# A planner's port waits between VectorE and GpSimd, its model of the DMA wires, and its due times

## The chip, the cores and the metric

One core of one Trainium2 chip. The metric is the device time of one execution in microseconds, the median of several runs. The engines are named as in the profile: PE is TensorE, PEld its weight loads, DVE is VectorE, ACT is ScalarE, POOL is GpSimd, SP is SyncE, which here only issues DMAs.

## What is computed

One layer of a hybrid encoder block on 512 tokens of width 1024, all in float32: three groups of attention heads behind one input projection, one output projection, a gated MLP with a causal convolution of width 3, and a gated per-layer embedding. Cut to what matters:

```python
def reference(x, p, ...):                       # x: (1, 512, 1024)
    h = x
    hn = rms_norm(h, ln_mix[0])
    z = hn @ w_in[0]                            # 1024 x 3590
    (q1, q2, k1, k2, va, qf, kf, vf, fg, qc, kc, vc) = split(z)
    # QK RMS norm of all heads, then
    o_a = diff_attention(q1, q2, k1, k2, va, lam, ...)   # 4 heads, two softmaxes each, ALiBi
    o_b = forgetting_attention(qf, kf, vf, log_f)        # 6 heads, cumulative log forget gate
    o_c = chunk_attention(qc, kc, vc, rel_bias)          # 6 heads, relative position bias
    h = h + concat([o_a, o_b, o_c]) @ w_out[0]
    h = h + conv_gated_mlp(rms_norm(h, ln_ffn[0]), w_up, conv_w, conv_b, w_down)   # d_ff 2816
    gate = sigmoid(rms_norm(h, ln_ple[0]) @ w_ple_gate[0])
    return h + (p[0] @ w_ple_proj[0]) * gate
```

## The kernel before

**Arithmetic.** Every float32 product is made of three fast ones: an operand is split into a rounded part (`whi`, `Th`, made by ScalarE with a cast) and the rest (`wlo`, `Tl`, made by DVE or POOL with a subtraction), and `mm3` issues hi*hi, hi*lo and lo*hi into one PSUM bank. So each weight tile of 128 x 768 takes a load by SP, a cast of ScalarE and a subtraction over two SBUF operands before PE can use it. The tiles stand in rings: 4 to 6 raw ones (`wraw`), 7 or 8 of `whi` and of `wlo`; a load waits until the subtraction has let go of the raw tile. Some sums of weights are made beforehand, on POOL by `tensor_tensor` (`sum_of`, line 1383) or by a POOL DMA that accumulates (`add_of`, line 1376).

**First part** (to line 1132, about the first 280 us): the input projection in ten parts of 4 token tiles, between them the attention of the pairs of heads. POOL has short steps in these chains: the power for the RMS norm (`rs`, in `qk_sums`, line 689), the moves of halves of `q` and `k` that scores wait for (`move`, line 712, called by `split_q` and `split_k`), the scaling of probabilities (`e`). DVE makes the splits, the masked scores with their minimum (`e` with its accumulator `st`, in `softmax_map`, line 852), reciprocals and evacuations. **Second part** (from line 1140): output projection's end, the MLP, with a saving of products for two blocks at a time that needs sums of weights and of activations (`up_seven`, line 1571; `down_weights`, line 1428), and the gate with the output.

**The planner.** Nothing is issued where it is written. While a plan is open (`PLAN`), every call on an engine becomes an `Op` of `Plan` (line 124) with the tiles that it reads and writes. `price` (line 184) gives it a duration; `op.port` (line 216) marks what uses the SBUF port that DVE and POOL share: every POOL operation but a DMA, and a DVE `tensor_scalar`, `tensor_tensor` or `scalar_tensor_tensor` with no operand in PSUM. `due` (line 225) gives PE operations due times by their place plus a shift of their group out of the table `SHIFT`, and from these, backwards, all others. `solve` (line 236) then plays the engines in time: at each step the engine that can start first takes the ready operation that is due first. `emit` (line 305) issues the operations in the order found; each engine runs its own in that order, and data dependencies become semaphores. All instructions therefore carry one line, L357, in the profile.

What the change touches in it:

- A port operation is planned only after the other engine's last one (`when`, line 247, over `held`). In the second plan POOL is planned 0.1 us later still (`late`, the fifth argument at line 1140), and in `emit` (line 313) a POOL operation over 0.6 us that follows a DVE port operation in the order gets a real semaphore wait on it (`behind`). The first plan (line 595) has `late` 0 and no such waits. DVE never waits for POOL on account of the port.
- DMAs share one wire in the plan, at 0.37 MB/us for those of SP, 0.105 for those of POOL, one after the other.
- `SURE` is 0.1: PE takes first what has been ready that long. `STICK` and `turns` keep transposes in bunches, and a lone transpose is charged 0.08 us.

Of the kernel before, what the change touches and what calls it, by code (L numbers as in the profile page):

```python
# [41 lines left out]
for _i in range(3):  # L42
# [5 lines left out]
AHEAD = 2  # L48
# [75 lines left out]
class Plan:  # L124
# [5 lines left out]
    def __init__(self, clock, there=(), mem=None, fresh=0.0, late=0.0):  # L130
        self.group, self.loaded, self.fresh, self.late = "first", set(), fresh, late
        self.clock, self.there, self.ops, self.mem = clock, [(v.tensor.name, self.region(v), t) for v, t in there], [], mem or {}

    @staticmethod
    def region(v):
        size = 2 if v.dtype == BF16 else 4
        (row, pn), *rest = [tuple(x) for x in v.ap]
        if v.tensor.space == bass.MemoryType.DRAM and v.tensor.name not in STAND_INS:
            return 0, 1, v.offset * size, (v.offset + (pn - 1) * row + sum((n - 1) * st for st, n in rest) + 1) * size
        p0, c0 = divmod(v.offset, row)  # L140
        return p0, p0 + pn, c0 * size, (c0 + sum((n - 1) * st for st, n in rest) + 1) * size
# [42 lines left out]
    def price(self, op):  # L184
# [4 lines left out]
        op.move, op.turns = 0, op.name == "transpose"  # L189
# [29 lines left out]
    LONG, STICK = 0.6, 2.0  # L219
    HW, SW, AT_ONCE = 0.37e6, 0.105e6, 8  # L220
    SURE, AHEAD, MUCH, WAIT = 0.1, 1.0, 2.0, 0.6
# [3 lines left out]
    def due(self, shift):  # L225
# [5 lines left out]
        for op in reversed(self.ops):  # L231
            if op.eng.name != "pe":
                spent = op.busy + op.lag + 0.05 + (op.move / self.HW + 2.0 if op.move else 0.0)
                op.dl = min([q.dl for q in op.next], default=t) - spent

    def solve(self):
# [6 lines left out]
        wire, out, order = 0.0, {"sp": [], "pool": []}, []  # L243
        turns, alone = False, False
        held = {"dve": 0.0, "pool": 0.0}
        other = {"dve": "pool", "pool": "dve"}
        when = lambda q: max(q.at, held[other[q.eng.name]] + (self.late if q.eng.name == "pool" else 0.0)) if q.port else q.at
        rank = lambda q: (q.dl, q.pos)
        while True:
            best = None  # L250
            for e in self.ENGINES:
                if free[e]:
                    t = max(clock[e], min(when(q) for q in free[e]))
                    if best is None or t < best[0]:
                        best = t, e
            if best is None:
# [3 lines left out]
            if e == "pe":  # L260
                can = [q for q in can if q.at + self.SURE <= t] or can
            op = min(can, key=rank)
            if e == "pe" and op.turns != turns:
                same = [q for q in can if q.turns == turns and q.dl < op.dl + self.STICK]
                if same and (turns or sum(q.turns and q.dl < op.dl + self.STICK for q in can) < 2 or min(q.dl for q in same) < op.dl + self.STICK / 2):
                    op = min(same, key=rank)
# [12 lines left out]
            if e == "pe":  # L279
                busy += 0.08 * (alone and not op.turns)  # L280
                turns, alone = op.turns, op.turns and not turns
            if op.move:
                done = out[e]
                if len(done) >= self.AT_ONCE:
                    t0 = max(t0, done[-self.AT_ONCE])
                wire = max(t0 + 2.0, wire) + op.move / (self.HW if e == "sp" else self.SW)
                op.end = wire + 0.6
                done.append(op.end)
# [7 lines left out]
            for q in op.next:  # L296
                q.left -= 1
                q.at = max(q.at, op.start if e == "pe" and q.eng is op.eng else op.end + self.LEAD[q.eng.name])
                if not q.left:
                    free[q.eng.name].append(q)  # L300
# [4 lines left out]
    def emit(self):  # L305
# [3 lines left out]
        before = None  # L309
        for op in self.choose():  # L310
            op.ins = op.eng.now(op.name, [real(v) for v in op.a], {q: real(v) for q, v in op.k.items()})
            if op.port:
                if before and op.eng.name == "pool" and before.eng.name == "dve" and op.busy > self.LONG and self.late:
# [1744 lines left out]
```

## Time and profile before

| | us |
|---|---|
| median of 3 runs | 708.28 |
| lowest and highest run | 708.25, 709.49 |
| the profiled execution | 707.89 |
| its span, first to last instruction | 706.0 |
| mean granted TensorE clock, share | 0.998 |

The span is shorter than the execution by what lies around the program. In the profile's views each row of a chain or timeline has its start and its length in us; x2 after a name merges two neighbours. A group's row has the busy time, the mean ns of one instruction, the idle time of its engine just before and what ended that. In a row of waits stand the total us, how many times, and the longest. A row by tile gives the shortest, median and longest instruction in ns.

### The profile page before, as it was taken

To read this page: it belongs to the slowest core of one execution; us is meant where nothing else is said; L and a number is where in the kernel's file an instruction comes from. 1 tells how busy PE (TensorE), PEld (TensorE's weight loads), DVE (VectorE), ACT (ScalarE), POOL (GpSimd) and SP (SyncE) were. 2 spreads that over 40 slices of the span, in tenths; PEclk is the share of its full clock that TensorE was granted. 3 is DMA by queue.
4 is the path that set the end of the run, shared out by engine and by line. 5 is a ranking of instruction groups with operands and counts; after the bars stand their busy time and mean duration, and the time that the engine had idled before them with its cause. 6 is when DMAs were issued, how large, how long until landed. Compare 5 with 4: busy or idle time off the path is not lost.

```text
span 706.0 us, 12402 instructions
## 1 busy us (share of the span) xinstructions
PE 690.3 (98%) x4420; PEld 636.4 (90%) x4420; DVE 552.5 (78%) x1126; ACT 408.7 (58%) x781; POOL 300.6 (43%) x403
## 2 busy tenths in 40 slices
PE   7999999999999999999999999999999999999997
PEld 7999999898999888899998999889988888999886
DVE  7679878879788666789888887997877998878722
ACT  6657676565766575666666435665345674536711
POOL 3788677766665452223223334304432203245200
PEclk9999999999999999999999999999999999999999
DMA  9523444423112252584763278651488552204521
GB/s 321 201 83 111 125 117 128 118 60 109 45 61 76 75 124 83 200 244 105 214 159 113 68 186 207 163 162 33 139 211 209 183 168 82 91 32 155 163 85 46
DMA packets 41275, 92.72 MB, mean 131 GB/s; under 512 B 4694, under 2 KB 7510, under 8 KB 41212
## 3 DMA queue, kind: packets, MB, share of 16 engines
q1 hardware_dynamic: 34572, 78.24, 33.1%
q0 software_dynamic: 6352, 13.38, 10.8%
q8 instruction: 35, 0.57, 0.3%
q10 hardware_dynamic: 288, 0.30, 0.1%
q14 instruction: 28, 0.23, 0.1%
HBM read 83.63 MB, written 4.21 MB: 124 GB/s over the span
## 4 chain that ended last, share of the span: by engine, by line
PE 91%; DVE 3%; DMA 2%; ACT 2%; POOL 1%; issue 1%; ACTq 0%; POOLq 0%
PE z L357 46%; PE s L357 22%; PE t L357 16%; PE o L357 7%; DMA wraw<-in_w_up_dram 1%; DVE wlo L357 1%; POOL k L357 1%; POOL q L357 1%; ACT whi L357 1%; DMA zn<-in_w_in_dram 0%; DVE e L357 0%; DVE conv L357 0%; POOL rs L357 0%; ACT e L357 0%; DVE kl L357 0%
## 5 line engine op out<-in xcount | busy, mean ns | idle before, releaser
L357 ACT CAST whi<-wraw 128x768 fp32r<-128x768 f32 (+2 forms) x140 | 106.1, 768 | 59.9 <-POOL wraw L357 11.4
L357 PE MATMUL z<-whi,Th 128*128 128x384 f32 (+2 forms) x356 | 123.4, 351 | 4.5 <-ACT whi L357 4.5
L357 DVE TENSOR_TENSOR wlo<-wraw,whi 128x768 fp32r<-128x768 f32 (+2 forms) x122 | 111.5, 930 | 15.4 <-ACT whi L357 13.6
L357 PE MATMUL z<-wlo,Th 128*128 128x384 f32 (+2 forms) x356 | 123.0, 350 | 0.0
L357 PE MATMUL z<-whi,Tl 128*128 128x384 f32 (+2 forms) x356 | 121.8, 347 | 0.0
L357 PEld LDWEIGHTS z<-whi,Th 128*128 128x128 f32 x356 | 66.9, 189 | 8.0 <-ACT whi L357 4.5
L357 POOL TENSOR_TENSOR wraw<-wraw,wraw 128x256 f32<-128x256 f32 (+1 forms) x22 | 28.3, 1285 | 101.3 <-DVE wlo L357 53.6
L357 PEld LDWEIGHTS z<-wlo,Th 128*128 128x128 f32 x356 | 67.2, 189 | 4.0 <-DVE wlo L357 0.4
L357 PEld LDWEIGHTS z<-whi,Tl 128*128 128x128 f32 x356 | 67.0, 189 | 3.8
L357 ACT ACTIVATE e<-e,st 128x128 f32<-128x128 f32 (+3 forms) x80 | 44.7, 560 | 29.8 <-DVE st L357 29.4
L357 PE MATMUL z<-Th,whi 128*128 128x512 f32 (+1 forms) x156 | 53.2, 346 | 1.4 <-ACT whi L357 1.3
L357 PE MATMUL s<-Th,whi 128*128 128x512 f32 (+1 forms) x156 | 53.3, 345 | 0.6 <-ACT whi L357 0.6
L357 PE MATMUL s<-Th,wlo 128*128 128x512 f32 (+1 forms) x156 | 53.7, 345 | 0.0
L357 PE MATMUL s<-Tl,whi 128*128 128x512 f32 (+1 forms) x156 | 53.6, 345 | 0.0
L357 PE MATMUL z<-Tl,whi 128*128 128x512 f32 (+1 forms) x156 | 53.5, 344 | 0.0
L357 PE MATMUL z<-Th,wlo 128*128 128x512 f32 (+1 forms) x156 | 53.4, 344 | 0.0
L357 POOL TENSOR_TENSOR rs<-rs,nhalf 128x4 f32<-128x4 f32 x40 | 43.5, 1091 | 4.8 <-DVE rs L357 2.3
L357 DVE CUSTOM_DVE_ANT_0 e<-s,bias 128x128 f32<-128x128 f32 (+3 forms) x74 | 33.7, 469 | 12.4 <-PE s L357 7.2
L357 DVE TENSOR_TENSOR conv<-conv,conv 128x512 f32<-128x512 f32 (+1 forms) x31 | 21.0, 691 | 24.0 <-ACT conv L357 23.8
L357 POOL TENSOR_SCALAR e<-e,st 128x512 f32<-128x512 f32 (+3 forms) x48 | 27.2, 576 | 18.1 <-DVE st L357 16.8
L357 PEld LDWEIGHTS z<-Th,whi 128*128 128x128 f32 x156 | 29.1, 188 | 4.8 <-ACT whi L357 1.8
L357 PEld LDWEIGHTS s<-Th,whi 128*128 128x128 f32 x156 | 29.2, 188 | 3.8 <-ACT whi L357 0.8
(352 smaller groups left out, 2152.4 us busy)
## 6 DMA issues: line engine op xcount, KB each, us to landing
wraw<-in_w_up_dram SPq DMA_DIRECT2D x41, 384.0 KB, 4.3
wraw<-in_w_in_dram SPq DMA_DIRECT2D x28, 384.0 KB, 3.7
wraw<-in_w_down_dram SPq DMA_DIRECT2D x16, 384.0 KB, 3.6
whi_again<-in_w_up_dram SPq DMA_DIRECT2D x11, 384.0 KB, 4.5
wraw<-in_w_out_dram SPq DMA_DIRECT2D x16, 256.0 KB, 2.7
wlo_again<-in_w_up_dram SPq DMA_DIRECT2D x10, 384.0 KB, 4.3
wraw<-in_w_up_dram SPq DMA_DIRECT2D x15, 256.0 KB, 4.1
wlo<-wraw POOLq DMA_DIRECT2D x7, 384.0 KB, 4.2
```

Source lines behind the costliest of these rows:

```text
L357: ins = getattr(self.eng, op)(*a, **k)
```

## The change

Both plans get semaphore waits in both directions. In `emit`, a port operation of either engine that lasts over 0.25 us waits for the last port operation that the builder has issued on the other engine before it, unless one of its engine already waited for that same one, and only if the plan starts it before that one's end plus `NEAR` (1.0 us for POOL, 0.6 for DVE). In `solve` a port operation is planned 0.2 us (POOL) or 0.1 us (DVE) after the other engine's end. The fifth argument of `Plan` is now `sure`, PE's margin of readiness: 0.15 in the first plan, still 0.1 in the second, whose call is unchanged. DMAs are played as two queues whose transfers are served in order, alone at 0.334 (SP) or 0.164 MB/us (POOL), at 0.143 and 0.078 when both are at work; at most 8 are on the way in a queue. The bunching of transposes and the charge for a lone one go. All values of `SHIFT` are new.

```diff
 SHIFT = {
-    "first": -11.4, "in1_0": -0.3, "in1_1": -25, "in1_2": -2.7, "A0a": -6.5, ...
+    "first": -23.2, "in1_0": -20, "in1_1": -10.4, "A0a": -14.9, ...
...
-    def __init__(self, clock, there=(), mem=None, fresh=0.0, late=0.0):
+    def __init__(self, clock, there=(), mem=None, fresh=0.0, sure=0.15):
...
-    LONG, STICK = 0.6, 2.0
-    HW, SW, AT_ONCE = 0.37e6, 0.105e6, 8
-    SURE, AHEAD, MUCH, WAIT = 0.1, 1.0, 2.0, 0.6
+    SHORT, HANDED, NEAR = 0.25, {"pool": 0.2, "dve": 0.1}, {"pool": 1.0, "dve": 0.6}
+    RATE = {("sp",): {"sp": 0.334e6}, ("pool",): {"pool": 0.164e6}, ("sp", "pool"): {"sp": 0.143e6, "pool": 0.078e6}}
+    SENT, ARRIVED, AT_ONCE = {"sp": 1.46, "pool": 1.49}, 0.58, 8
+    AHEAD, MUCH, WAIT = 1.0, 2.0, 0.6
...
-        when = lambda q: max(q.at, held[other[q.eng.name]] + (self.late if q.eng.name == "pool" else 0.0)) if q.port else q.at
+        def when(q):
+            if q.port:
+                return max(q.at, held[other[q.eng.name]] + self.HANDED[q.eng.name])
+            if q.move:
+                return max(q.at, gate[q.eng.name]) if len(wire[q.eng.name]) < self.AT_ONCE else never
+            return q.at
...
+        def landed(until):
+            nonlocal now
+            while now < until:
+                busy = tuple(e for e in wire if wire[e] and wire[e][0][1] <= now)
+                rate = self.RATE.get(busy, {})
...
-                can = [q for q in can if q.at + self.SURE <= t] or can
+                can = [q for q in can if q.at + self.sure <= t] or can
             op = min(can, key=rank)
-            if e == "pe" and op.turns != turns:
-                same = [q for q in can if q.turns == turns and q.dl < op.dl + self.STICK]
...
-            if e == "pe":
-                busy += 0.08 * (alone and not op.turns)
-                turns, alone = op.turns, op.turns and not turns
...
-                if before and op.eng.name == "pool" and before.eng.name == "dve" and op.busy > self.LONG and self.late:
-                    op.eng.behind(op.ins, before.ins)
-                before = op
+                e = op.eng.name
+                d = last["pool" if e == "dve" else "dve"]
+                if d and d is not known[e] and op.busy > self.SHORT and op.start < d.start + d.busy + self.NEAR[e]:
+                    op.eng.behind(op.ins, d.ins)
+                    known[e] = d
+                last[e] = op
```

More of the change, by code (lines that the diff above doesn't have):

```diff
@@ L128 @@
     LEAD = {"act": 0.035, "dve": 0.035, "pool": 0.095, "pe": 0.055, "sp": 0.1}
-    def __init__(self, clock, there=(), mem=None, fresh=0.0, late=0.0):
-        self.group, self.loaded, self.fresh, self.late = "first", set(), fresh, late
+    def __init__(self, clock, there=(), mem=None, fresh=0.0, sure=0.15):
+        self.sure = sure
+        self.group, self.loaded, self.fresh = "first", set(), fresh
         self.clock, self.there, self.ops, self.mem = clock, [(v.tensor.name, self.region(v), t) for v, t in there], [], mem or {}
@@ L137, in region @@
         (row, pn), *rest = [tuple(x) for x in v.ap]
-        if v.tensor.space == bass.MemoryType.DRAM and v.tensor.name not in STAND_INS:
+        if v.tensor.space == bass.MemoryType.DRAM and v.tensor.name not in STAND_INS and v.tensor.name != "out_dram":
             return 0, 1, v.offset * size, (v.offset + (pn - 1) * row + sum((n - 1) * st for st, n in rest) + 1) * size
@@ L188, in price @@
         acc = "accum_out" in k
-        op.move, op.turns = 0, op.name == "transpose"
+        op.move = 0
         if e == "pe":
@@ L232, in due @@
             if op.eng.name != "pe":
-                spent = op.busy + op.lag + 0.05 + (op.move / self.HW + 2.0 if op.move else 0.0)
+                spent = op.busy + op.lag + 0.05 + (op.move / 0.37e6 + 2.0 if op.move else 0.0)
                 op.dl = min([q.dl for q in op.next], default=t) - spent
@@ L242, in solve, with release @@
                 free[op.eng.name].append(op)
-        wire, out, order = 0.0, {"sp": [], "pool": []}, []
-        turns, alone = False, False
+        wire, now, gate, order = {"sp": [], "pool": []}, 0.0, {"sp": 0.0, "pool": 0.0}, []
         held = {"dve": 0.0, "pool": 0.0}
         other = {"dve": "pool", "pool": "dve"}
-        when = lambda q: max(q.at, held[other[q.eng.name]] + (self.late if q.eng.name == "pool" else 0.0)) if q.port else q.at
+        never = 1e18
+        def when(q):
[4 more added lines that the diff above has]
+            return q.at
+        def release(op, e):
+            for q in op.next:
+                q.left -= 1
+                q.at = max(q.at, op.start if e == "pe" and q.eng is op.eng else op.end + self.LEAD[q.eng.name])
+                if not q.left:
+                    free[q.eng.name].append(q)
+        def landed(until):
[3 more added lines that the diff above has]
+                rate = self.RATE.get(busy, {})
+                step, who = until - now, None
+                for e in wire:
+                    if e in rate and wire[e][0][2] / rate[e] <= step:
+                        step, who = wire[e][0][2] / rate[e], e
+                    if wire[e] and e not in rate and wire[e][0][1] - now < step:
+                        step, who = wire[e][0][1] - now, None
+                now = until if step == until - now else now + step
+                for e in rate:
+                    wire[e][0][2] -= rate[e] * step
+                if who:
+                    op = wire[who].pop(0)[0]
+                    op.end = now + self.ARRIVED
+                    if len(wire[who]) + 1 >= self.AT_ONCE:
+                        gate[who] = op.end
+                    return op, who
+            return None
         rank = lambda q: (q.dl, q.pos)
@@ L255, in solve @@
                         best = t, e
+            there = landed(best[0] if best else never) if wire["sp"] or wire["pool"] else None
+            if there:
+                release(*there)
+                continue
             if best is None:
@@ L260, in solve @@
             if e == "pe":
-                can = [q for q in can if q.at + self.SURE <= t] or can
+                can = [q for q in can if q.at + self.sure <= t] or can
             op = min(can, key=rank)
-            if e == "pe" and op.turns != turns:
-                same = [q for q in can if q.turns == turns and q.dl < op.dl + self.STICK]
-                if same and (turns or sum(q.turns and q.dl < op.dl + self.STICK for q in can) < 2 or min(q.dl for q in same) < op.dl + self.STICK / 2):
-                    op = min(same, key=rank)
             if e not in ("pe", "sp"):
@@ L278, in solve @@
             busy = op.busy * (1.85 if e == "pe" and t0 < 8.6 else 1.0)
-            if e == "pe":
-                busy += 0.08 * (alone and not op.turns)
-                turns, alone = op.turns, op.turns and not turns
             if op.move:
[L283 to L288, printed above, removed]
+                wire[e].append([op, t0 + self.SENT[e], op.move])
             else:
@@ L295, in solve @@
             order.append(op)
[L296 to L300, printed above, removed]
+            if not op.move:
+                release(op, e)
         assert len(order) == len(self.ops)
@@ L308, in emit @@
                 d.next.append(op)
-        before = None
+        last, known = {"dve": None, "pool": None}, {"dve": None, "pool": None}
         for op in self.choose():
```

75 rows, old and new, of the table SHIFT are left out of this document.

## The prediction

> **What bounds the kernel now.** I read the page first, then the chain that ended last, then the waits of TensorE (PE) alone, then two halves of the span.
>
> ```profile
> span 706.0 us, 12402 instructions
> PE 690.3 (98%) x4420; PEld 636.4 (90%) x4420; DVE 552.5 (78%) x1126; ACT 408.7 (58%) x781; POOL 300.6 (43%) x403
> ```
> ```profile
> PE 91%; DVE 3%; DMA 2%; ACT 2%; POOL 1%; issue 1%; ACTq 0%; POOLq 0%
> ```
>
> PE is busy for 690.3 of 706.0 us and carries 91% of the chain. So no edit on another engine is worth more than the 15.7 us in which PE is idle, and most of that is out of reach, as the next view shows.
>
> ```profile
> PE z L357 <- ACT whi L357: 5.8, 2, 4.5
> PE s L357 <- POOL k L357: 2.1, 3, 1.3
> PE s L357 <- DVE st L357: 1.3, 2, 1.1
> PE s L357 <- ACT whi L357: 0.6, 1, 0.6
> PE t L357 <- DVE kl L357: 0.2, 1, 0.2
> PE t L357 <- DVE ptl L357: 0.2, 1, 0.2
> PE t L357 <- issue: 0.2, 1, 0.2
> ```
>
> Columns: total us, times, longest. The 4.5 is the start, before the first weights are there; no edit touches it. What lies behind PE's last matmul isn't in this list either. The change can win only the rest: 1.3 + 2.1 + 1.3 + 0.6 + 0.6 = 5.9 us. That is the ceiling, 0.8% of the span.
>
> Two of these waits are collisions of VectorE (DVE) and GpSimd (POOL). First the chain of work around the longest wait for POOL k, the DVE's timeline beside it, and the same POOL operation over the whole run:
>
> ```profile
> 121.78 1.99 POOL q L357
> 123.78 0.59 POOL k L357
> 124.37 0.04 issue
> 124.41 0.74 PE s L357 x4
> ```
> ```profile
> 122.36 0.94 DVE L357 TENSOR_TENSOR wlo<-wraw,whi 128x768 fp32r<-128x768 f32 x1
> ```
> ```profile
> L357 POOL TENSOR_SCALAR q<-ql x20: 611/616/1994, 36.6 to 256.4; 64x512 fp32r<-64x512 f32 x20
> ```
>
> A move of the median 616 ns took 1.99 us, and it ended 0.47 us after DVE's weight split (122.36 + 0.94 = 123.30), though it had begun 0.58 us ahead of it. The scores waited for the next move behind it. The second case is the longest wait for DVE st:
>
> ```profile
> 155.13 3.83 DVE wlo L357 x2
> 158.96 0.26 DVE e L357
> ...
> 159.28 0.73 PE s L357 x2
> ```
> ```profile
> 155.98 2.15 POOL L357 TENSOR_TENSOR wlo<-wraw,whi 128x768 fp32r<-128x768 f32 x1
> ```
> ```profile
> L357 DVE TENSOR_TENSOR wlo<-whi_again,whi 128x768 fp32r<-128x768 f32 x18 | 17.2, 954 | 3.1 <-ACT whi L357 3.0
> ```
>
> The last row is from the groups by shape; its 954 is the mean ns of one split. Two of them should take 1.9 us; beside a POOL subtraction of 2.15 us they took 3.83. So each engine holds the other, in both directions. A third place shows that POOL can lose several times in a row:
>
> ```profile
> 32.27 3.45 POOL L357 TENSOR_TENSOR rs<-rs,nhalf 128x4 f32<-128x4 f32 x1 [0.97 <-DVE rs L357]
> ```
> ```profile
> 32.16 2.69 DVE L357 TENSOR_TENSOR wlo<-wraw,whi 128x768 fp32r<-128x768 f32 x3
> ```
> ```profile
> L357 POOL TENSOR_TENSOR rs<-rs,nhalf x40: 1002/1018/3447, 26.9 to 232.3; 128x4 f32<-128x4 f32 x40
> ```
>
> A power of 1018 ns took 3447, until all three back-to-back splits were through.
>
> **The change, part by part.** *Waits between the two engines.* Until now only a POOL operation over 0.6 us waits, only in the second part, only right behind a DVE port operation. Now each engine's port operation over 0.25 us waits for the other's last one in the builder's order, in both parts, if the plan has it start soon after. It removes no work and adds no pass over data. It decides who goes first: the DVE split at 122.36, if planned behind the moves, no longer overtakes them, and the scores at 124.41 lose their 1.3; the split at 155 either runs first or leaves its place to `e`, and the 1.1 goes. The rest of the POOL k group is 0.8; I take half of it, 0.4, since nothing in the list says which of the two shorter waits come from a held move. Together 1.3 + 1.1 + 0.4 = 2.8. Bounds: 0 (the order stays as it is) and 3.4 (all of both groups).
>
> What a wait costs by itself comes from handoffs that are there already:
>
> ```profile
> 154.59 0.16 DVE L357 RECIPROCAL st<-st 128x1 f32<-128x1 f32 x1 [1.14 <-ACT e L357]
> 154.85 0.37 POOL L357 TENSOR_SCALAR e<-e,st 128x128 f32<-128x128 f32 x1 [0.32 <-DVE st L357]
> ```
> ```profile
> 286.16 0.58 POOL L357 TENSOR_TENSOR rstd<-rstd,nhalf 128x1 f32<-128x1 f32 x1
> 286.77 0.75 DVE L357 SCALAR_TENSOR_TENSOR conv<-h,rstd,pin 128x512 f32<-128x512 f32 x1 [0.35 <-POOL rstd L357]
> ```
>
> From DVE to POOL 154.85 - 154.75 = 0.10 us, from POOL to DVE 286.77 - 286.74 = 0.03. The rule waits at most once for any one operation, so with 403 POOL instructions DVE gets at most 403 new waits, 12 us, against 706.0 - 552.5 = 153.5 us idle; POOL's at most 403 come to 40 us against 405 idle. As sums they are hidden. Uncovered, on a chain such as POOL q, k, PE s, one costs its 0.1.
>
> The dear part is what stands behind a waiting DVE instruction. The DVE runs in order; behind a split that waits for POOL stand the `e` and `st` of the next scores, for which ScalarE and PE wait, and the next split, for which SP's loads wait (SP's waits, then the first 280 us; columns of the latter: PE, weight loads, DVE, ScalarE, POOL, clock, DMA share, GB/s):
>
> ```profile
> SPq L357 <- DVE wlo L357: 304.0, 122, 14.7
> ```
> ```profile
> 0.00:280.00 280.00, 271.56 (x1648) 254.40 (x1649) 219.19 (x629) 180.37 (x427) 177.05 (x275) 1.00 0.37 113
> ```
>
> In the first 280 us DVE has 61 us idle and POOL is busy 177 of 280, so a wait there has cover only if the plan is right about POOL. I charge three new small waits of PE of 0.3 each, +0.9: the handoff's 0.1 and the 0.2 that the shorter wait for DVE st lasts (1.3 - 1.1). Bounds: nothing, and the 1.1 of a real hold at each of some places, which is the rival below.
>
> *Wire rates.* The planner now lets a hardware and a GpSimd queue share the wire and slow each other. The place where this matters is the 0.6 us wait for whi, behind a weight load that the chain shows:
>
> ```profile
> 538.98 5.21 DMA wraw<-in_w_up_dram
> ```
> ```profile
> wraw<-in_w_up_dram SPq DMA_DIRECT2D x41, 384.0 KB, 4.3
> ```
>
> It landed 0.9 us later than the median. Knowing this, the planner can only issue earlier or take PE work in another order, and SP's 304 us of waiting for splits says that a load goes out when a buffer comes free, no sooner. So I count half of the two later whi waits, (1.3 + 0.6) / 2 = 0.9 as a gain; bounds 0 and 1.9, and a loss of one more such wait, 1.3.
>
> *Transposes no longer bunched, and no charge for a lone one.* The rows around a lone transpose, and a bunch of three:
>
> ```profile
> 43.20 0.28 PE L357 MATMUL s<-kl,q 128*128 128x256 f32 x1
> 43.31 0.27 PE L357 MATMUL t<-ident,zn 128*128 128x128 f32 x1
> 43.34 0.42 PE L357 MATMUL z<-whi,Th 128*128 128x384 f32 x1
> 43.60 0.34 PE L357 MATMUL z<-wlo,Th 128*128 128x384 f32 x1
> 43.78 0.34 PE L357 MATMUL z<-whi,Tl 128*128 128x384 f32 x1
> ```
> ```profile
> 122.44 0.49 PE L357 MATMUL t<-ident,e 128*128 128x128 f32 x3
> ```
>
> From 43.20 to 43.60 are 0.40 us. A 384-wide step takes 43.78 - 43.60 = 0.18, the 256-wide one 43.31 - 43.20 = 0.11, which leaves 0.11 for the transpose. In the bunch, with the lone one's 0.27 for the last, one takes (0.49 - 0.27) / 2 = 0.11 as well. So splitting bunches costs nothing that I can see; I take 0. *The readiness margin of 0.15 instead of 0.1 in the first part and the new due times* only reorder; their cost is in the three waits above.
>
> Sum: 707.89 (the profiled execution, 706.0 of it span) - 2.8 - 0.9 + 0.9 = 705.1. The median of the three runs, 708.28, lies 0.39 above the profiled execution, so the forecast is **705.5 us**.
>
> **Rivals.** *The waits only rename the blocking.* Both engines already exclude each other; if the builder's order is the order that happens anyway, or the thresholds catch few of the held pairs, a held instruction becomes a waiting one and PE's list stays: 708.3, at most 0.4 less or more for handoffs. Against it speaks that the move begun at 121.78 was overtaken. [...]
>
> *DVE is held behind a late POOL operation (slower).* A fixed order can't use it when POOL comes late: DVE stands with ready work behind it. Its price is the row at 155: 1.9 us of hold made 1.1 us of PE wait. POOL has 275 instructions in the first 280 us; if six of the waits for them (one in 46) end like this, the time is 708.3 - 2.8 + 6.6 = 712.1; with seven, 713.2. It decides from three on, whose 3.3 eats the 2.8. For it speaks DVE's 78% there (219.19 of 280); against it that nearly all moves and powers keep to their medians (616, 1018), so that the plan can know when POOL is done.
>
> *More than I count goes.* If the new plan clears the whole list, 708.3 - 5.9 = 702.4.
>
> **How the numbers follow.** This kernel's runs can tell about 0.2%, 1.4 us: faster is under 706.9, slower over 709.7. Forecast 0.42; the list cleared 0.10 (0.04 of it under 702.4); renaming 0.12; DVE held 0.36, of which 0.08 over 713.2. So faster 0.52, same 0.12, slower 0.36, and the range 702.4 to 713.2 leaves out 0.12. The forecast's own range is 703.9 to 706.9.
>
> **What would show it.** Right: stretched POOL moves and powers fall to their medians (616, 1018 ns) and DVE's splits to 954; PE's waits for POOL k and DVE st fall from 3.4 to about 1; lone transposes still cost 0.11. Wrong: new lines in which DVE waits for POOL, followed by PE waiting for DVE st, zn or wlo; SP's wait for splits above 304 us; a wait of PE for whi over 1.3. If the list shrinks and the time doesn't, the tail or PE's order took it back.

## The result, and the profile after

| | before | after |
|---|---|---|
| median, us | 708.26 (6 runs, 707.39 to 709.49) | 715.95 (6 runs, 711.46 to 717.21) |
| profiled execution, us | 707.89 | 715.94 |
| its span, us | 706.0 | 714.2 |

The kernel got slower: ratio 1.0098, interval 1.0082 to 1.0114. It is the side of the second rival, above its 712.1.

First the page's head of the changed kernel (all its instructions carry line L386):

```profile
span 714.2 us, 12433 instructions
PE 696.9 (98%) x4420; PEld 639.2 (90%) x4420; DVE 543.6 (76%) x1126; ACT 409.7 (57%) x781; POOL 277.9 (39%) x403
```

DVE is busy 8.9 us less and POOL 22.7 us less than before, for the same instructions: the two no longer hold each other. PE does the same 4420 matmuls and is busy 6.6 us *more*; its idle time rose only from 15.7 to 17.3. So the loss must be looked for inside PE's busy time too. The waits of PE, without the start and four rows of 0.2 or 0.3 (columns: total us, times, longest):

```profile
PE s L386 <- ACT conv L386: 2.9, 1, 2.9
PE t L386 <- DVE wlo L386: 1.3, 1, 1.3
PE z L386 <- ACT Th L386: 0.8, 2, 0.7
PE t L386 <- DVE ptl L386: 0.8, 1, 0.8
PE z L386 <- DVE Tl L386: 0.6, 1, 0.6
PE s L386 <- DVE st L386: 0.5, 2, 0.3
```

The wait for POOL k (2.1) is gone, that for DVE st fell from 1.3 to 0.5, and the later waits for whi (1.3 and 0.6) are gone. In their place stand waits that the kernel before did not have. Now by place. For each matmul I took the time from its start to the start of the next one, less what it takes in an unbroken row (0.117 us for 256 columns, 0.175 for 384, other widths in proportion, 0.109 for a transpose), and summed this by stretch. It is worked out from all of PE's rows in the timeline, so it also holds pauses that are too short for the list of waits:

| stretch, us | before | after |
|---|---|---|
| 0 to 120 | 4.3 | 7.1 |
| 120 to 160 | 4.4 | 1.5 |
| 160 to 280 | 0.6 | 1.7 |
| 280 to 360 | -0.1 | 2.3 |
| 360 to 440 | 0.8 | 0.5 |
| 440 to 480 | 0.0 | 5.1 |
| 480 to 560 | 3.0 | 2.6 |
| 560 to the end | 0.5 | 1.9 |
| all | 13.7 | 22.7 |

The whole difference is 9.0 us; the span grew by only 8.2, because what lies behind PE's last matmul got shorter, from 5.3 to 4.4 us. (The change also has the planner track the output in DRAM by region, in a line that the diff above doesn't show; what shortened the end was not tried.) The stretch with the two collisions that the prediction named gained 2.9. Five of the other seven lose, 360 to 440 and 480 to 560 gain a little; the dearest is 440 to 480. There the timeline shows, POOL first, then DVE, ScalarE and PE (start, length, engine and operation, in brackets the idle time before and what ended it):

```profile
449.71 0.87 POOL L386 DMA_DIRECT2D wraw<-in_w_up_dram  x1 [0.37 <-issue]
454.35 0.73 POOL L386 TENSOR_TENSOR wraw<-wraw 128x256 f32<-128x256 f32 x1 [3.77 <-DMA wraw<-in_w_up_dram]
...
455.11 1.53 DVE L386 SCALAR_TENSOR_TENSOR conv<-conv,cols,conv 128x511 f32<-128x511 f32 x2 [4.75 <-POOL wraw L386]
...
457.28 1.01 ACT L386 CAST ah<-conv 128x512 fp32r<-128x512 f32 x2 [3.22 <-DVE conv L386]
458.62 0.39 PE L386 MATMUL s<-Th,whi 128*128 128x256 f32 x1 [2.85 <-ACT conv L386]
```

Read from the top: a POOL DMA that adds a weight tile to another goes out at 449.71. POOL's next sum needs it and stands 3.77 us. DVE's convolution needs none of these weights, only the turn that the new wait gives it; it stands 4.75 us until POOL's 0.73 us sum is done. ScalarE stands behind the convolution, and PE waits 2.9 us for ScalarE's rounded part. And then the bill goes on. The same execution in short windows (window, its length, PE, weight loads, DVE, ScalarE, POOL busy with counts, granted clock, DMA share, GB/s):

```profile
454.00:458.00 4.00, 1.76 (x13) 1.33 (x12) 2.85 (x5) 0.78 (x3) 0.73 (x1) 1.00 0.50 99
460.00:461.00 1.00, 1.00 (x7) 1.00 (x7) 0.77 (x1) 0.00 (x0) 1.00 (x2) 0.65 0.87 335
461.00:462.00 1.00, 1.00 (x7) 1.00 (x6) 1.00 (x4) 0.00 (x0) 0.02 (x1) 0.50 0.32 30
462.00:463.00 1.00, 1.00 (x7) 1.00 (x7) 0.20 (x1) 0.82 (x1) 0.00 (x0) 0.50 0.89 119
463.00:464.00 1.00, 1.00 (x5) 0.86 (x5) 0.96 (x1) 0.76 (x3) 0.00 (x0) 0.64 1.10 289
464.00:466.00 2.00, 2.00 (x16) 1.83 (x15) 1.30 (x3) 1.51 (x4) 0.84 (x2) 1.00 0.71 213
```

About 1.7 us after PE went on, TensorE's granted clock fell to a half, and from 460.4 on a 256-column step took 0.21 us instead of 0.117. PE counts as wholly busy there and does less: (1 - 0.65) + 0.50 + 0.50 + (1 - 0.64) = 1.7 us lost, so an estimated 1.7 / 0.5 = 3.4 us at half the clock, with no row in the list of waits. The hold cost 2.9 + 1.7, near the 5.1 of this stretch. In e7 below, where DVE doesn't stand behind this sum, the same count gives 0.5 for the stretch.

How often the new waits keep DVE standing behind POOL shows in DVE's list:

```profile
DVE wlo L386 <- POOL wlo_again L386: 7.3, 5, 2.8
DVE wlo L386 <- POOL wraw L386: 5.7, 4, 3.6
DVE conv L386 <- POOL wraw L386: 4.8, 1, 4.8
DVE pin L386 <- POOL wraw L386: 2.6, 2, 1.4
```

These 20.4 us have no counterpart before. All four lines are waits for sums of weights in the second part. Besides the one above, those that seem to reach PE lie at 314, 320 and 543 us: the waits for Tl (0.6), Th (0.7) and wlo (1.3) follow soon after them. No wait in PE's list stands behind the 3.6 at 491 us.

### The profile page after: what moved, and what is told of

The parts are those of the page before. It is cut to its first block, busy times and chain, and to the rows that moved or that the text cites. A ratio compares the mean times of both kernels' runs of the same rounds, so it can differ in the third digit from the quotient of the medians.

```text
span 714.2 us, 12433 instructions
## 1 busy us (share of the span) xinstructions
PE 696.9 (98%) x4420; PEld 639.2 (90%) x4420; DVE 543.6 (76%) x1126; ACT 409.7 (57%) x781; POOL 277.9 (39%) x403
## 5 line engine op out<-in xcount | busy, mean ns | idle before, releaser
L386 ACT CAST whi<-wraw 128x768 fp32r<-128x768 f32 (+2 forms) x140 | 105.8, 769 | 47.5 <-PE s L386 13.3
L386 PE MATMUL z<-whi,Th 128*128 128x384 f32 (+2 forms) x356 | 124.0, 357 | 5.0 <-ACT whi L386 4.5
L386 PE MATMUL z<-wlo,Th 128*128 128x384 f32 (+2 forms) x356 | 122.3, 352 | 0.4 <-DVE V L386 0.3
L386 PE MATMUL z<-whi,Tl 128*128 128x384 f32 (+2 forms) x356 | 122.1, 351 | 0.0
L386 DVE TENSOR_TENSOR wlo<-wraw,whi 128x768 fp32r<-128x768 f32 (+2 forms) x122 | 104.6, 879 | 19.6 <-ACT whi L386 9.6
L386 PEld LDWEIGHTS z<-whi,Th 128*128 128x128 f32 x356 | 67.0, 190 | 9.9 <-ACT whi L386 4.5
L386 PEld LDWEIGHTS z<-wlo,Th 128*128 128x128 f32 x356 | 66.8, 189 | 4.9 <-DVE wlo L386 0.5
L386 PEld LDWEIGHTS z<-whi,Tl 128*128 128x128 f32 x356 | 66.9, 189 | 3.6
L386 PE MATMUL s<-Th,whi 128*128 128x512 f32 (+1 forms) x156 | 54.0, 347 | 2.9 <-ACT conv L386 2.9
L386 PE MATMUL z<-Tl,whi 128*128 128x512 f32 (+1 forms) x156 | 53.6, 346 | 0.6 <-DVE Tl L386 0.6
L386 PE MATMUL z<-Th,whi 128*128 128x512 f32 (+1 forms) x156 | 53.4, 345 | 0.7 <-ACT Th L386 0.7
L386 PE MATMUL s<-Tl,whi 128*128 128x512 f32 (+1 forms) x156 | 53.8, 346 | 0.0
L386 PE MATMUL s<-Th,wlo 128*128 128x512 f32 (+1 forms) x156 | 53.7, 348 | 0.0
L386 PE MATMUL z<-Th,wlo 128*128 128x512 f32 (+1 forms) x156 | 53.6, 345 | 0.0
L386 ACT ACTIVATE e<-e,st 128x256 f32<-128x256 f32 (+3 forms) x80 | 44.7, 561 | 14.7 <-DVE st L386 14.1
L386 POOL TENSOR_TENSOR wraw<-wraw,wraw 128x256 f32<-128x256 f32 (+1 forms) x22 | 27.1, 1241 | 65.5 <-DVE wlo L386 39.7
L386 POOL TENSOR_TENSOR rs<-rs,nhalf 128x4 f32<-128x4 f32 x40 | 40.7, 1019 | 19.9 <-DVE wlo L386 10.1
L386 DVE CUSTOM_DVE_ANT_0 e<-s,bias 128x384 f32<-128x384 f32 (+3 forms) x74 | 33.7, 470 | 8.9 <-PE s L386 7.8
L386 PEld LDWEIGHTS s<-Th,whi 128*128 128x128 f32 x156 | 29.6, 190 | 6.9 <-ACT conv L386 3.7
L386 DVE TENSOR_TENSOR conv<-conv,conv 128x512 f32<-128x512 f32 (+1 forms) x31 | 20.4, 670 | 19.1 <-ACT conv L386 18.8
L386 PEld LDWEIGHTS z<-Th,whi 128*128 128x128 f32 x156 | 29.2, 188 | 4.3 <-ACT Th L386 0.9
L386 PEld LDWEIGHTS z<-Tl,whi 128*128 128x128 f32 x156 | 29.2, 188 | 4.0 <-DVE Tl L386 0.8
```

What stands on the lines that cost most here:

```text
L386: ins = getattr(self.eng, op)(*a, **k)
```

## The experiments

Two theories stood at the start: the new waits cost, because they hold DVE behind POOL sums that come late (in the expectations W); and the new order costs, while the waits only rename a blocking that is there anyway (O). The first runs refuted a half of each. What was left of W, a case of the second rival, is called L from e7 on: the dear holds of DVE are those behind sums that wait for a DMA. The letter F, later, stands for due times that fit only the rules with which they came. The medians stand beside the kernel before on the same chips, 708.4 to 708.6.

| run | what differs | median, us | ratio to before, interval |
|---|---|---|---|
| e1 | after, no port waits | 728.09 | 1.0264 (1.0239 to 1.0288) |
| e2 | after, waits in the first part only | 725.65 | 1.0229 (1.0203 to 1.0254) |
| e3 | after, only POOL waits | 712.97 | 1.0064 (1.0046 to 1.0083) |
| e4 | before's order, all new waits | 706.73 | 0.9967 (0.9952 to 0.9982) |
| e5 | before, without its own waits | 737.85 | 1.0409 (1.0373 to 1.0445) |
| e6 | before's order, only POOL waits | 707.19 | 0.9981 (0.9966 to 0.9996) |
| e7 | after, DVE not behind POOL sums fed by a DMA | 710.21 | 1.0022 (1.0005 to 1.0038) |
| h1 | old first plan, new second, all waits | 712.97 | 1.0051 (1.0023 to 1.0078) |
| h2 | new first plan, old second, all waits | 711.34 | 1.0036 (1.0024 to 1.0047) |
| h3 | h1 with the rule of e7 | 708.81 | 1.0008 (0.9988 to 1.0028) |
| e12 | e4 with the rule of e7 | 705.71 | 0.9962 (0.9949 to 0.9975) |
| e13 | after, the accumulating DMAs a quarter as large | 707.48 | 0.9988 (0.9971 to 1.0006) |
| e14 | after, POOL's transfers planned 2 us later | 736.28 | 1.0393 (1.0359 to 1.0427) |
| e15 | after, first plan's margin 0.1 | 740.46 | 1.0451 (1.0405 to 1.0496) |
| e16 | e4, new due times in the first plan | 729.03 | 1.0292 (1.0254 to 1.0329) |

### Waits or order

The first four change only the rule in `emit`; the order of each engine's instructions stays.

```diff
 # e1: if False and d and ...      e2: if self.fresh == 0.0 and d and ...
-                if d and d is not known[e] and op.busy > self.SHORT and ...
 # e3
+                if e == "pool" and d and d is not known[e] and op.busy > self.SHORT and ...
 # e4: the kernel before, with the rule of the change in place of its own
+                if d and d is not known[e] and op.busy > self.SHORT and op.start < d.start + d.busy + self.NEAR[e]:
+                    op.eng.behind(op.ins, d.ins)
+                    known[e] = d
```

> The changed kernel's order, with no port wait at all. Theory W (DVE is held by the new waits behind POOL sums of weights that themselves wait for an accumulating DMA, and PE runs dry behind it): the four waits of PE in the second part that follow such a hold (2.9, 1.3, 0.7, 0.6 us) go, some collisions come back, so 708 to 711 us. Theory O (the new due times and PE's order are the loss, the waits only rename a blocking that the port makes anyway): 714 to 717 us.

> The changed kernel's order with the new waits in the first plan alone. Theory W: the second part gets its 5 to 6 us back, the first keeps its clean port, 709 to 711 us, with DVE waiting for POOL wraw and wlo_again nowhere over 1 us. Theory O: 714 to 717 us.

> The changed kernel's order, POOL waits for DVE as changed, DVE never waits for POOL. Theory W: 709 to 711 us, since only DVE's waits hold the loads, the casts and PE. Theory O: 714 to 717 us.

> The kernel before, its own plan and order, with the changed kernel's rule of waits in both parts. Theory W: slower than before, 711 to 716 us, with DVE waits for POOL over 1 us in the second part. Theory O: within 1 us of before, 707 to 709.

The waits as a whole are not the loss. Without them (e1, e2) the new order is far slower than either theory said, so they don't just rename a blocking; e3 lies between the two guesses, and e4 just under the one of O. On the old order they win 1.9 us; on the new one they win 12 (728.1 to 716.0), of which the first part's 2.4 (728.1 to 725.7) and the second's the rest. Given the same waits, the new order costs 716.0 - 706.7 = 9.2 us. So the order is the loss, with one exception: in the new order DVE's waits do more harm than good (e3 is 3.0 faster than after, though the two intervals just touch). The longest waits of PE in e4:

```profile
PE s L361 <- ACT whi L361: 1.5, 2, 0.9
PE s L361 <- POOL k L361: 0.9, 2, 0.7
```

The wait of 1.3 for POOL k and that of 1.1 for DVE st are gone here too, as predicted; of POOL k two shorter ones stay, and whi's 1.9 became 1.5.

The kernel before without its own POOL waits, and with POOL waits alone:

```diff
 # e5
-                    op.eng.behind(op.ins, before.ins)
+                    pass
 # e6: e4 with
+                if e == "pool" and d and ...
```

> The kernel before, its order, with its own POOL waits of the second part taken away. Theory C (collisions on the port in the second part are dear whatever the order: a POOL sum of 1.85 us holds DVE): 711 to 718 us. Rival (only the new order needs waits; the old one was laid out without them): 708 to 709.5 us.

> The kernel before, its order, the new rule for POOL's waits in both parts, no wait of DVE. If DVE's waits cost 3 us in any order, as they do in the new one (716.0 against 713.0 without them): 703 to 705 us. If in the old order it is they that bring the 1.9 us: 707.5 to 709 us. Between these (706 to 707) they do nothing here.

I had not thought the collisions so dear. The few waits that the kernel before already had are worth 29 us to it. In e5, PE's longest groups of waits and two groups by shape (busy time, mean ns of one, idle time before):

```profile
PE t L357 <- DVE h L357: 8.0, 4, 3.9
PE t L357 <- DVE wlo L357: 3.9, 3, 2.0
```
```profile
L357 DVE TENSOR_TENSOR wlo<-whi_again,whi 128x768 fp32r<-128x768 f32 x18 | 24.0, 1335 | 3.1 <-ACT whi L357 3.0
L357 POOL TENSOR_TENSOR wraw<-wraw,wraw 128x768 f32<-128x768 f32 x10 | 21.0, 2107 | 67.9 <-DVE wlo L357 67.9
```

The same split took 954 ns in the kernel before, the sum 1847. Both stand in the stretch where POOL makes its long sums of weights; PE then waits up to 3.9 us for a sum of activations (h). Not all of the 29 us comes directly from instructions that stretch each other: the mean granted clock of e5's profiled execution was 0.986, which over 738.0 us makes an estimated 10.3 us lost, against 1.4 in the kernel before (0.998 of 706.0). DVE's waits add nothing that can be told on the old order: e6 and e4 overlap.

### Which POOL operations hold DVE

In e7 DVE doesn't wait for a POOL operation that itself hangs on a DMA; POOL still waits for DVE everywhere.

```diff
-                if d and d is not known[e] and ...
+                if d and not (e == "dve" and self.loads(d)) and d is not known[e] and ...
+    def loads(self, d):
+        return any(q.move or q.eng.name == "pool" and self.loads(q) for q in d.deps)
```

> The changed kernel, its order, but DVE doesn't wait for a POOL operation whose data come by a DMA, directly or over another POOL operation. Theory L (the dear holds of DVE are those behind late landings): 711 to 713.5 us, like the kernel without any wait of DVE or better, and no wait of DVE for POOL wraw or wlo_again over 1 us. Rival (every wait of DVE costs its handoff): 714.5 to 716.5 us.

5.7 us come back, a little more than expected, with every engine in the order of the changed kernel. DVE's list has none of the four lines left, and PE's no wait for ACT conv, Th or Tl. Its longest, without the start:

```profile
PE t L389 <- DVE ptl L389: 1.9, 1, 1.9
PE t L389 <- ACT whi L389: 0.9, 1, 0.9
PE t L389 <- DVE h L389: 0.7, 1, 0.7
```

So the hold of DVE is the cause of these 5.7. The other waits of DVE are worth having here: e7 is 2.8 faster than e3, where DVE never waits. Nor is it the sum of the holds that costs. In e4 DVE's list has 44 us of waiting for POOL, in the changed kernel 29, and for sums of weights 15 against 21; but in e4 none of the latter is longer than 1.9 us, and leaving them out (e12, below) won 1.0 us, which can't be told from nothing.

Whether the sums are late because their DMAs land late is another question. The views of DMA issues show them slow (size, median us from issue to landing), first before, then after:

```profile
wraw<-in_w_up_dram POOLq DMA_DIRECT2D x6, 256.0 KB, 4.3
wraw<-in_w_up_dram POOLq DMA_DIRECT2D x6, 128.0 KB, 4.5
whi_again<-in_w_up_dram POOLq DMA_DIRECT2D x3, 128.0 KB, 5.4
```
```profile
wraw<-in_w_up_dram POOLq DMA_DIRECT2D x6, 256.0 KB, 7.3
wraw<-in_w_up_dram POOLq DMA_DIRECT2D x6, 128.0 KB, 5.0
whi_again<-in_w_up_dram POOLq DMA_DIRECT2D x3, 128.0 KB, 7.2
```

By the constants of the diff the new planner lands 128 KB after 1.49 + 128 x 1024 / 0.164e6 + 0.58 = 2.87 us if POOL's queue has the wire alone, and after 3.75 at its shared rate of 0.078, when nothing stands before it in its queue. The old one took 2.0 + 1.25 + 0.6 = 3.85, and more when the one wire was busy. The rows after say 5.0 and 7.2. So they land later than planned. Most also land later than before, though not all: those of 256 KB into whi_again took 6.3 before and 5.5 after. So e13 shortens the accumulating DMAs of `add_of` to 32 of 128 partitions, while the plan still takes them for whole: three quarters of those sums are left out, each engine's order is kept.

```diff
-            op.move = n * 4 * op.outs[0].shape[0]
+            op.move = n * 4 * (128 if e == "pool" and op.outs[0].shape[0] == 32 else op.outs[0].shape[0])
...
-            pool.dma_start(out=w.t[:, c0:c1], in_=src(), accum_op=ALU.add)
+            pool.dma_start(out=w.t[:32, c0:c1], in_=src()[:32], accum_op=ALU.add)
```

> The changed kernel in its own order, with one difference: every accumulating POOL DMA of a sum of weights moves 32 of the 128 partitions, so three quarters of those sums are left out; the plan is kept as if the DMAs were whole. Theory L (DVE is held because these DMAs land later than planned): they land at least 2 us earlier than the 5.0 to 7.3 us of the changed kernel, DVE's waits for POOL wraw and wlo_again fall from 20 us to under 6, PE's wait for ACT conv (2.9) is gone, and the time is 710 to 712, as where DVE didn't wait for those POOL operations (710.2). If the time from issue to landing is mostly fixed, or if the holds come from another delay: the waits stay and the time is 715 to 717.

```profile
wraw<-in_w_up_dram POOLq DMA_DIRECT2D x6, 64.0 KB, 4.0
wraw<-in_w_up_dram POOLq DMA_DIRECT2D x6, 32.0 KB, 3.0
```

They land 2.0 and 3.3 us earlier, PE's wait for ACT conv is gone, and the time falls by 8.5 us, more than the change had lost (7.7). DVE's convolution waits 1.9 us for its sum instead of 4.8. So the late landing is a cause of the holds, and that of the dearest. Two things are not as expected. DVE's waits for these sums, the same four lines, fell only from 20.4 to 11.9 us (the one of 3.6 stayed as it was), and the time fell by more than e7's 5.7. With POOL's accumulating DMAs a quarter as large SP's loads land earlier as well (its 256 KB loads of wraw in 3.9 us instead of 5.8), so that the surplus of 2.7 need not be the hold's.

In e14 the planner is told the later landing:

```diff
-    SENT, ARRIVED, AT_ONCE = {"sp": 1.46, "pool": 1.49}, 0.58, 8
+    SENT, ARRIVED, AT_ONCE = {"sp": 1.46, "pool": 3.5}, 0.58, 8
```

> The changed kernel, with the planner's delay before a POOL transfer starts set from 1.49 to 3.5 us, so that a lone sum of 128 KB is planned to land after 4.9 us instead of 2.9 and one of 256 KB after 5.7 instead of 3.7: near the 5.0 and 7.3 measured. Only the order in the second part changes. Theory L (the optimistic landing is what costs): DVE's waits for POOL wraw and wlo_again fall from 20 us to under 8, and the time is 709 to 713. Theory F (the due times are fitted to the planner's own model, and any change of the model undoes the fit): the holds fall, but PE waits elsewhere, 714 to 719.

The time is theory F's, and worse than it said: a later landing with the same due times loses 20 us. The holds hardly fell: DVE's waits for POOL wraw and wlo_again are still 16 us, not under 8. And the order changed in the first part too, from PE's 253rd matmul on; PE does 1537 matmuls in the first 280 us, where it did 1644. So e14 tests neither side of L. It shows that the due times of that table make a good order only with the constants beside them.

### Which plan, which rule

h1 and h2 hold both planners, each with its due times and its rules, and let one make each part; the waits are those of the change throughout. h3 and e12 add the rule of e7.

```diff
 # h1; h2 the other way round
+class OldPlan:                     # the planner before, with its SHIFT and the new emit
-    PLAN.append(Plan({"act": 2.95, "dve": 0.9, "pool": 3.9, "sp": 0.73, "pe": 1.0}, ...
+    PLAN.append(OldPlan({"act": 2.95, "dve": 0.9, "pool": 3.9, "sp": 0.73, "pe": 1.0}, ...
```

> First part planned as before (old due times, wires, bunches), second as changed, the new rule of waits in both. The old plan with these waits takes 706.7, the new one 716.0. If the loss lies in the second part's plan: 713 to 716 us. If in the first part's: 707 to 710 us. Theory L says the second, since its sums wait for accumulating DMAs: 712 to 715.

> First part planned as changed, second as before, the new rule of waits in both. The other way round took 713.0 with waits, so the first part's plan has 716.0 - 713.0 = 3.0 of the loss and the second's 713.0 - 706.7 = 6.2. If the parts add up: 709 to 711 us. If the second part's loss came from what the new first part leaves behind (its ring places, its clocks): 713 to 716 us.

> First part planned as before, second as changed, DVE not waiting for POOL operations fed by a DMA. Theory L, sums of the two effects: 713.0 - 5.7 = 707 us, 706 to 708.5, that is nothing of the second part's plan but the holds was dear. Rival (the new second plan has a loss of its own besides the holds): 709.5 to 713 us.

> The kernel before, its order, the new rule of waits in both parts but DVE not behind POOL operations fed by a DMA. Theory L with the old plan's pessimistic landings (its holds behind POOL sums are at most 1.9 us and PE has none of them on its list): the same as with all waits, 706 to 707.5 us. If these holds are dear here too: 703 to 705.5 us.

Of the 9.2 us of the new order the second plan makes 713.0 - 706.7 = 6.2 with the old first plan (h1 against e4) or 716.0 - 711.3 = 4.6 with the new one (after against h2), the first plan the other 3.0 or 4.6; so the parts don't add up quite, and h1's runs lie between 710.0 and 715.8. With the rule of e7 on both orders, the new one is still 710.2 - 705.7 = 4.5 dearer (e7 against e12): about half of the 9.2 is the holds, the other half is not explained. The second plan alone keeps 708.8 - 705.7 = 3.1 of it (h3 against e12), between the two guesses, but h3's runs lie between 705.6 and 713.1, so its size is loose. e12 is the fastest of all and beats both kernels; it lies between its two guesses, and from e4 it can't be told.

Two runs ask what in the first plan costs:

```diff
 # e15: after
-    def __init__(self, clock, there=(), mem=None, fresh=0.0, sure=0.15):
+    def __init__(self, clock, there=(), mem=None, fresh=0.0, sure=0.1):
 # e16: e4, and the groups of the first plan with the new values
-    "first": -11.4, "in1_0": -0.3, "in1_1": -25, "in1_2": -2.7, "A0a": -6.5, ...
+    "first": -23.2, "in1_0": -20, "in1_1": -10.4, "A0a": -14.9, "in1_3": -3.7, ...
```

> The changed kernel with PE's margin of readiness in the first plan back at 0.1 us. If the margin of 0.15 is what makes the new first plan dearer by 3 to 4.6 us: 711.5 to 713. If it isn't: 715 to 717; above 717 if the wider margin was itself a gain.

> The kernel before with the new waits (706.7), its old wires, bunches and margin, and only the new due times in the first plan. If the due times of the first plan are what costs 3 to 4.6 us: 709.5 to 711.5. If the cost is in the planner's rules of the first plan (margin, planned handoff, no bunches): 706 to 708. The due times stand here with rules to which they weren't fitted, so that a result above 711.5 says only that they don't suit each other.

Both lie far above the ranges, where the expectations say least: that the wider margin is a gain with the rest of its plan, and that the new due times don't suit the old rules. With 0.05 us less margin, the changed kernel loses 24.5 us. The windows of the first 280 us, after and e15:

```profile
0.00:280.00 280.00, 272.92 (x1644) 255.17 (x1644) 214.82 (x626) 179.03 (x424) 159.79 (x272) 1.00 0.39 113
```
```profile
0.00:280.00 280.00, 258.93 (x1510) 237.30 (x1511) 199.37 (x583) 166.68 (x393) 150.32 (x251) 0.98 0.36 107
```

PE does 134 matmuls fewer in that time. The margin, the rates and the due times can't be priced one by one: e14, e15 and e16 each take one of them from its partners and lose 20 to 25 us, more than the whole change. So it stays open which of them makes the new first plan 3 to 4.6 us dearer; that would need due times found anew for each set of rules, which was not tried.

## Why the prediction was wrong

*The step that failed* is the last of the parts: the margin and the new due times "only reorder; their cost is in the three waits above". Reordering was the largest term. At equal waits the new order costs 9.2 us (after against e4), and 4.5 of it stay when DVE doesn't stand behind sums fed by a DMA (e7 against e12); the prediction had nothing for it, and less than nothing with the wire rates. What in the order makes these 4.5 stays open. The diff said that every due time was new; from the trace of before the worth of an order can't be read, and the range should have said so.

*The ceiling* was broken by no run (the fastest, e12, gained 2.8), but it isn't shown, and it says nothing of a loss. It took PE's busy time as given, yet that went from 690.3 to 703.9 us in e5, for the same matmuls. And it read the list of waits as all that PE loses. Of the 9.0 us by which starts lie further apart, the list without the start shows 7.9 - 5.9 = 2.0 (the 7.9 include the four rows left out above). Half of the 9.0, about 4.5 us, lies in pauses between 30 and 200 ns, which the list hardly shows: by the same count some 40 of them before and twice as many after, the steps at the slow clock (1.7) among them. How many one counts depends on how the shift between a transpose and its neighbours is evened out; the difference hardly does.

*The waits, -2.8*: right in mechanism, place and size where it was named. 120 to 160 us gained 2.9, in e4 with the old order about as much (down to about 1.7), and POOL's moves and powers keep to their medians, as was said:

```profile
L386 POOL TENSOR_SCALAR q<-ql x20: 614/617/622, 45.9 to 260.9; 64x512 fp32r<-64x512 f32 x20
```
```profile
L386 POOL TENSOR_TENSOR rs<-rs,nhalf x40: 1001/1019/1037, 26.4 to 236.2; 128x4 f32<-128x4 f32 x40
```

For the kernel as a whole e4 gives 1.9, so about one came back elsewhere. That the waits only rename the blocking is refuted by e4 and, far more plainly, by e1 and e5.

*Three small waits of PE, +0.9*: the kind was right, the size wrong by a factor of six. DVE's holds behind POOL cost 5.7 us (e7); they are part of the 9.2, since the old order hardly pays for them (e12 against e4). The second rival described this: DVE stands with ready work behind a late POOL operation. It was placed in the first 280 us, where DVE is fullest. It came in the second part, where POOL waits for its own DMAs. There POOL's waits for DMAs, before and after, said it:

```profile
POOL wraw L357 <- DMA wraw<-in_w_up_dram: 19.5, 7, 7.7
```
```profile
POOL wraw L386 <- DMA wraw<-in_w_up_dram: 53.2, 16, 10.3
```

A view of before had this row, 7.7 us at its longest. I had read POOL's waits as cover, not as a delay that DVE would inherit. The rival's price, 1.1 us of PE for 1.9 of hold, was fair for short holds (1.3 for 2.8 at 543 us); the long hold paid 2.9 and the clock's 1.7.

*Wire rates, -0.9*: not shown. Both later whi waits went, worth 1.9, but the 1.3 went in e12 too, which plans with the old rates. The new rates let POOL's sums land too early in the plan, and the dearest hold came from a late landing (e13). Whether it came from the rates or from the due times stays open, since no run has the one without the other.

*Transposes, 0*: right. Rows of PE around a lone one, after:

```profile
44.72 0.34 PE L386 MATMUL z<-whi,Tl 128*128 128x384 f32 x1
44.89 0.34 PE L386 MATMUL z<-whi,Th 128*128 128x384 f32 x1
45.07 0.27 PE L386 MATMUL t<-ident,zn 128*128 128x128 f32 x1
45.09 0.42 PE L386 MATMUL z<-wlo,Th 128*128 128x384 f32 x1
45.36 0.38 PE L386 MATMUL t<-ident,zn 128*128 128x128 f32 x2
```

From 44.89 to 45.36 are 0.47 us for two 384-wide steps (0.175 each, by 44.72 to 45.07) and one transpose, which leaves 0.12 for it; the prediction had 0.11.

*Of the signs* in "What would show it", most came true on both sides. PE's waits for POOL k and DVE st fell from 3.4 to 0.5, and DVE waits for POOL with PE waiting behind it. The list shrank in its old places and the time didn't; the last sentence there names what took it back, PE's order. SP's wait for splits did not grow:

```profile
SPq L386 <- DVE wlo L386: 301.6, 123, 18.8
```

## What to carry to other kernels

Before an in-order engine is made to wait for another's operation, ask what that operation itself waits for: one fed by a DMA passes the DMA's delay on, to work that has nothing to do with it (POOL's 3.77 us for its DMA became 4.75 us of DVE and 2.85 of PE). On the old order it was enough that POOL waits for DVE (707.2, with both 706.7). Where DVE waits too, leave out its waits on whatever hangs on a transfer: on the new order that gave 710.2, against 716.0 with all waits and 713.0 with none of DVE's. When a change brings new planner constants together with new due times, treat the order as the largest unknown: try the old order with the new waits first, and change no single constant under due times that were made with another.

## What the runs showed of the hardware

**Pauses of PE can cost twice.** The clock fell to 0.50 after the pause of 2.85 us above, and also after one of 1.83 us in e13, which ended at 194.03:

```profile
192.00:194.00 2.00, 0.20 (x2) 0.00 (x0) 2.00 (x6) 1.61 (x6) 1.64 (x3) 1.00 0.00 0
194.00:195.00 1.00, 0.97 (x6) 0.97 (x7) 0.72 (x4) 0.00 (x0) 0.64 (x2) 0.85 0.00 0
195.00:197.00 2.00, 2.00 (x8) 2.00 (x7) 2.00 (x3) 0.00 (x0) 0.00 (x0) 0.50 0.05 6
```

In e7 nearly the same pause, 1.92 us, stands in the same place, and the clock did not fall:

```profile
193.41 0.33 PE L389 MATMUL t<-ident,zn 128*128 128x128 f32 x1 [1.92 <-DVE ptl L389]
```
```profile
195.00:197.00 2.00, 2.00 (x14) 2.00 (x13) 1.98 (x3) 0.00 (x0) 0.00 (x0) 1.00 0.34 75
```

So the length of the pause alone doesn't decide it, 1.83 us with a fall and 1.92 without; what does was not shown. Whether the spread of the changed kernel's runs, 711.5 to 717.2, comes from this was not tried; the mean granted clock alone doesn't sort them (0.999 in the fastest, 0.998 in the slowest, 0.994 in one of 715.95).

**Running DVE and POOL side by side without an order** is dear. For the same instructions in the same order, without the waits that the kernel before had, DVE's busy time rose from 552.5 to 583.2 us in e5 and POOL's from 300.6 to 315.5, and the kernel lost 29, some 9 of them by the clock (10.3 - 1.4, the estimate above). Beside a DVE operation with an operand in PSUM no such stretch shows: DVE's `h<-h,t`, whose `t` is a PSUM tile, took 680 to 689 ns in all 25 cases after, and POOL's sum at 634.30, with two of them under way beside it, took 1.86 us where the mean is 1.85. That what DVE and POOL share is a port of SBUF is the planner's picture; the runs show which operations stretch each other and by how much.
